# Rotary embedding on one core: the first and last rows move as f32 on SyncE's queue, and the positions come in four small transfers

## Chip, core and metric

The kernel runs on one core of a Trainium2 chip. The metric is the device time of one execution in microseconds, the median of three runs. The profile shows one execution; its span is a little shorter than the device time, because some of the launch and the end lies outside it.

## What is computed

`x` holds 8 x 8 heads of 1024 positions with 64 features in f32. Each position turns the two halves of its features by an angle, position times frequency:

```python
half = x.shape[-1] // 2                       # 32
angles = np.outer(positions, freqs)           # 1024 x 32
cos, sin = np.cos(angles), np.sin(angles)
x_first, x_second = x[..., :half], x[..., half:]
out_first  = x_first * cos - x_second * sin
out_second = x_first * sin + x_second * cos
```

The input is 16.8 MB of f32 and so is the output. The table of angles is small (1024 x 32) and is the same for all 64 heads.

## The kernel before

A partition holds 64 consecutive positions (`C = 64`) of one head, so 16 partitions (`chunks`) hold a head and a tile of 128 partitions holds 8 heads. There are 8 tiles (`ntiles`). A row of a tile is one position with its 64 features. Each partition's part of a tile is one run of 64 x 64 x 4 B = 16 KB in memory.

The transfers of `x` are issued by GpSimd, and they convert f32 to bf16 on the way in and bf16 to f32 on the way out. All eight loads are issued at once; each tile has buffers of its own.

```python
pos_i = singles.tile([P, C, 1], positions.dtype)
nc.sync.dma_start(out=pos_i, in_=...)      # positions, repeated for 8 groups of 16 partitions
fr = singles.tile([P, half], f32)
nc.scalar.dma_start(out=fr, in_=freqs[None, :].to_broadcast([P, half]))

xts = []
for g in range(ntiles):
    xt = xpool.tile([P, C, d], bf16)
    nc.gpsimd.dma_start(out=xt.rearrange("p c d -> p (c d)"), in_=hbm(x, g))
    xts.append(xt)
```

VectorE and ScalarE build the tables of sine and cosine, `sin_h` and `cos_h`, in bf16. The angle is counted in turns, the whole turns are taken off, and ScalarE applies the sine:

```python
nc.vector.tensor_copy(out=pos_f, in_=pos_i.bitcast(mybir.dt.int32)[:, :, :1])
...
nc.vector.tensor_mul(out=turns, in0=pos_f..., in1=fturn...)      # 128 x 2048, f32
nc.vector.tensor_scalar(out=whole, in0=turns, ...)               # rounded to whole turns
nc.vector.tensor_sub(out=turns, in0=turns, in1=whole)
nc.scalar.activation(out=sin_h, in_=turns, func=Sin, scale=twopi)
nc.scalar.activation(out=whole, in_=turns, func=Abs)
nc.scalar.activation(out=cos_h, in_=whole, func=Sin, scale=-twopi, bias=half_pi)
```

Then each tile takes six VectorE operations, and its store is issued by GpSimd:

```python
for g in range(ntiles):
    ...
    v.tensor_mul(out=t1, in0=xf, in1=sin_h)
    v.tensor_mul(out=t2, in0=xs, in1=sin_h)
    v.tensor_mul(out=of, in0=xf, in1=cos_h)
    v.tensor_mul(out=os_, in0=xs, in1=cos_h)
    v.tensor_sub(out=of, in0=of, in1=t2)
    v.tensor_add(out=os_, in0=os_, in1=t1)
    nc.gpsimd.dma_start(out=hbm(out, g), in_=ot.rearrange("p c d -> p (c d)"))
```

Of the kernel before, what the change touches and what calls it, by code (L numbers as in the profile page):

```python
# [2 lines left out]

# [4 lines left out]


@with_exitstack  # L10
def kernel(
    ctx: ExitStack,
    tc: tile.TileContext,
    x: bass.AP,
    freqs: bass.AP,
    positions: bass.AP,
    out: bass.AP,
):
    nc = tc.nc
    f32 = mybir.dt.float32  # L20
    bf16 = mybir.dt.bfloat16
    Sin = mybir.ActivationFunctionType.Sin
    Alu = mybir.AluOpType

    b, h, seq, d = x.shape
    bh = b * h
    half = d // 2
    P = 128
    twopi = 2 * math.pi


    C = 64
    chunks = seq // C
    group = P // chunks
    ntiles = bh // group
    run = C * d
    assert chunks * C == seq and group * chunks == P and ntiles * group == bh

    singles = ctx.enter_context(tc.tile_pool(name="singles", bufs=1))
    xpool = ctx.enter_context(tc.tile_pool(name="xin", bufs=ntiles))  # L40
    opool = ctx.enter_context(tc.tile_pool(name="xout", bufs=ntiles))
    tpool = ctx.enter_context(tc.tile_pool(name="tmp", bufs=2))

    def hbm(t, g):
        return bass.AP(tensor=t.tensor, offset=t.offset + g * P * run, ap=[[run, P], [1, run]])


    pos_i = singles.tile([P, C, 1], positions.dtype)
    nc.sync.dma_start(
        out=pos_i,  # L50
        in_=bass.AP(tensor=positions.tensor, offset=positions.offset,
                    ap=[[0, group], [C, chunks], [1, C]]))
    fr = singles.tile([P, half], f32)
    nc.scalar.dma_start(out=fr, in_=freqs[None, :].to_broadcast([P, half]))


    xts = []
    for g in range(ntiles):
        xt = xpool.tile([P, C, d], bf16)
        nc.gpsimd.dma_start(out=xt.rearrange("p c d -> p (c d)"), in_=hbm(x, g))  # L60
        xts.append(xt)


    half_pi = singles.tile([P, 1], f32)
    nc.vector.memset(half_pi, math.pi / 2)  # L65
    pos_f = singles.tile([P, C, 1], f32)
    nc.vector.tensor_copy(out=pos_f, in_=pos_i.bitcast(mybir.dt.int32)[:, :, :1])  # L67
    fturn = singles.tile([P, 1, half], f32)
    nc.vector.tensor_scalar_mul(out=fturn[:, 0, :], in0=fr, scalar1=1.0 / twopi)  # L69
    turns = singles.tile([P, C, half], f32)  # L70
    nc.vector.tensor_mul(out=turns, in0=pos_f.to_broadcast([P, C, half]),  # L71
                         in1=fturn.to_broadcast([P, C, half]))
    whole = singles.tile([P, C, half], f32)
    magic = 1.5 * 2.0 ** 23
    nc.vector.tensor_scalar(out=whole, in0=turns, scalar1=magic, scalar2=magic,  # L75
                            op0=Alu.add, op1=Alu.subtract)
    nc.vector.tensor_sub(out=turns, in0=turns, in1=whole)  # L77
    sin_h = singles.tile([P, C, half], bf16)
    cos_h = singles.tile([P, C, half], bf16)
    nc.scalar.activation(out=sin_h, in_=turns, func=Sin, scale=twopi)  # L80

    nc.scalar.activation(out=whole, in_=turns, func=mybir.ActivationFunctionType.Abs)  # L82
    nc.scalar.activation(out=cos_h, in_=whole, func=Sin, scale=-twopi, bias=half_pi)  # L83

    v = nc.vector
    for g in range(ntiles):
        xt = xts[g]
        xf = xt[:, :, :half]
        xs = xt[:, :, half:]
        ot = opool.tile([P, C, d], bf16)  # L90
        of = ot[:, :, :half]
        os_ = ot[:, :, half:]
        t1 = tpool.tile([P, C, half], bf16)
        t2 = tpool.tile([P, C, half], bf16)
        v.tensor_mul(out=t1, in0=xf, in1=sin_h)  # L95
        v.tensor_mul(out=t2, in0=xs, in1=sin_h)  # L96
        v.tensor_mul(out=of, in0=xf, in1=cos_h)  # L97
        v.tensor_mul(out=os_, in0=xs, in1=cos_h)  # L98
        v.tensor_sub(out=of, in0=of, in1=t2)  # L99
        v.tensor_add(out=os_, in0=os_, in1=t1)  # L100
        nc.gpsimd.dma_start(out=hbm(out, g), in_=ot.rearrange("p c d -> p (c d)"))  # L101


# [1 line left out]
_INS = ['x', 'freqs', 'positions']  # L105
_OUTS = [((8, 8, 1024, 64), 'float32')]


# [23 lines left out]
```

## Time and profile before

| what | value |
|---|---|
| device time | 86.46 us (86.45 to 86.51) |
| span of the profiled execution | 84.2 us |
| VectorE busy | 60.7 us in 54 instructions |
| ScalarE busy | 7.0 us |
| GpSimd busy (issuing transfers) | 8.9 us |
| one VectorE operation on a tile, 128x2048 bf16 | 1.22 us |
| loads, stores | 8 of each, all on GpSimd's queue |
| read from memory, written to memory | 16.86 MB, 16.78 MB |

How to read it: the engines run side by side, so the busy times do not add up. VectorE is ahead of its stores, which stand in a queue; a wait of an engine matters only if what it waits for is on the path that sets the end. The transfers' bytes are counted on the side they are written to, so a converting load counts 1 MB for 2 MB read. "To landing" is the time from the issue of a transfer to the signal that all of it has arrived, so it includes the time that it stood in the queue.

### The profile page before, as it was taken

What the parts mean: (1) busy time and instruction counts of PE and PEld (TensorE: products, weight loads), DVE (VectorE), ACT (ScalarE), POOL (GpSimd) and SP (SyncE); (2) the same over time, 40 slices, a digit from 0 to 9 for tenths busy, and PEclk for the clock granted to TensorE, in tenths of its full rate; (3) what the DMA queues carried; (4) which work ended last, traced back from release to release, by engine and by line L of the source; (5) the groups of instructions that cost most, each with busy time, mean ns of one, the idle gap of its engine ahead of it and who ended that gap; (6) DMA issues with size and microseconds to landing.
All of it is one profiled execution on the core that took longest, in us unless ns stands there. A gap on an engine that the chain in (4) does not pass through costs nothing.

```text
span 84.2 us, 132 instructions
## 1 busy us (share of the span) xinstructions
DVE 60.7 (72%) x54; ACT 7.0 (8%) x4; POOL 8.9 (11%) x20
## 2 busy tenths in 40 slices
DVE  0069927999999999999999999999999910000000
ACT  4100079900000000000000000000000000000000
POOL 5960000000201100200200200100020020000000
DMA  0399999999999999999999999999999999999990
GB/s 2 60 210 214 214 218 218 214 214 214 214 222 210 218 218 210 218 218 214 210 342 405 459 405 467 381 490 381 482 389 467 405 451 420 428 443 405 467 373 0
DMA packets 2584, 25.25 MB, mean 300 GB/s; under 512 B 408, under 2 KB 536, under 8 KB 536
## 3 DMA queue, kind: packets, MB, share of 16 engines
q0 software_dynamic: 2304, 25.17, 97.2%
q1 hardware_dynamic: 136, 0.07, 0.3%
q10 hardware_dynamic: 144, 0.02, 0.1%
HBM read 16.86 MB, written 16.78 MB: 399 GB/s over the span
## 4 chain that ended last, share of the span: by engine, by line
issue 65%; DMA 10%; POOL 4%; POOLq 1%; PEldq 0%
DMA xt<-in_x_dram 10%; POOL out_dram L101 4%; POOLq L127 1%; POOLq L101 0%; PEldq L127 0%
## 5 line engine op out<-in xcount | busy, mean ns | idle before, releaser
L95 DVE TENSOR_TENSOR t<-xt,sin_h 128x2048 bf16<-128x2048 bf16 x8 | 9.8, 1224 | 2.0 <-ACT sin_h L80 2.0
L101 POOL DMA_DIRECT2D out_dram<-ot x8 | 4.3, 535 | 58.6 <-DVE ot L100 58.6
L99 DVE TENSOR_TENSOR ot<-ot,t 128x2048 bf16<-128x2048 bf16 x8 | 9.8, 1225 | 0.0
L97 DVE TENSOR_TENSOR ot<-xt,cos_h 128x2048 bf16<-128x2048 bf16 x8 | 9.8, 1224 | 0.0
L100 DVE TENSOR_TENSOR ot<-ot,t 128x2048 bf16<-128x2048 bf16 x8 | 9.8, 1224 | 0.0
L98 DVE TENSOR_TENSOR ot<-xt,cos_h 128x2048 bf16<-128x2048 bf16 x8 | 9.8, 1223 | 0.0
L96 DVE TENSOR_TENSOR t<-xt,sin_h 128x2048 bf16<-128x2048 bf16 x8 | 9.8, 1223 | 0.0
L60 POOL DMA_DIRECT2D xt<-in_x_dram x8 | 4.4, 578 | 0.8 <-PEq L127 0.8
L67 DVE CAST pos_f<-pos_i 128x64 f32<-128x64 int32 x1 | 0.2, 196 | 4.1 <-DMA pos_i<-in_positions_dram 4.1
L80 ACT ACTIVATE sin_h<-turns 128x2048 bf16<-128x2048 f32 x1 | 1.9, 1911 | 8.7 <-DVE turns L77 8.7
L77 DVE TENSOR_TENSOR turns<-turns,whole 128x2048 f32<-128x2048 f32 x1 | 2.3, 2293 | 0.0
L71 DVE TENSOR_TENSOR turns<-pos_f,fturn 128x2048 f32<-128x2048 f32 x1 | 2.3, 2291 | 0.0
L83 ACT ACTIVATE cos_h<-whole,half_pi 128x2048 bf16<-128x2048 f32 x1 | 2.0, 2003 | 0.0
L82 ACT ACTIVATE whole<-turns 128x2048 f32<-128x2048 f32 x1 | 1.9, 1896 | 0.0
L80 ACT ACT_TABLE_LOAD x1 | 1.3, 1283 | 1.1 <-PEq L116 1.1
L75 DVE TENSOR_SCALAR whole<-turns 128x2048 f32<-128x2048 f32 x1 | 1.2, 1226 | 0.0
L65 DVE MEMSET half_pi<- 128x1 f32 x1 | 0.1, 59 | 0.8 <-PEq L116 0.8
L69 DVE TENSOR_SCALAR fturn<-fr 128x32 f32<-128x32 f32 x1 | 0.2, 174 | 0.0
L116 POOL MEMSET const-float32-0.0<- 128x1 f32 x1 | 0.1, 99 | 0.2 <-issue 0.2
L116 POOL MEMSET const-bfloat16-1.0<- 128x1 bf16 x1 | 0.1, 102 | 0.0
L116 POOL MEMSET const-float32-1.0<- 128x1 f32 x1 | 0.1, 99 | 0.0
L116 POOL MEMSET const-uint8-127<- 128x1 uint8 x1 | 0.1, 99 | 0.0
## 6 DMA issues: line engine op xcount, KB each, us to landing
out_dram<-ot POOLq DMA_DIRECT2D x8, 2048.0 KB, 21.7
xt<-in_x_dram POOLq DMA_DIRECT2D x8, 1024.0 KB, 23.6
pos_i<-in_positions_dram SPq DMA_DIRECT2D x1, 64.0 KB
fr<-in_freqs_dram ACTq DMA_DIRECT2D x1, 16.0 KB, 3.6
```

The lines of the kernel that those rows point to most:

```text
L60: nc.gpsimd.dma_start(out=xt.rearrange("p c d -> p (c d)"), in_=hbm(x, g))
L71: nc.vector.tensor_mul(out=turns, in0=pos_f.to_broadcast([P, C, half]), in1=fturn.to_broadcast([P, C, half]))
L77: nc.vector.tensor_sub(out=turns, in0=turns, in1=whole)
L80: nc.scalar.activation(out=sin_h, in_=turns, func=Sin, scale=twopi)
L83: nc.scalar.activation(out=cos_h, in_=whole, func=Sin, scale=-twopi, bias=half_pi)
L95: v.tensor_mul(out=t1, in0=xf, in1=sin_h)
L96: v.tensor_mul(out=t2, in0=xs, in1=sin_h)
L97: v.tensor_mul(out=of, in0=xf, in1=cos_h)
L98: v.tensor_mul(out=os_, in0=xs, in1=cos_h)
L99: v.tensor_sub(out=of, in0=of, in1=t2)
L100: v.tensor_add(out=os_, in0=os_, in1=t1)
L101: nc.gpsimd.dma_start(out=hbm(out, g), in_=ot.rearrange("p c d -> p (c d)"))
```

## The change

The change moves three things. The first 16 rows of every partition of tile 0 (the head) are loaded as f32 on SyncE's queue, in two transfers with 2 KB runs, and ScalarE converts them to bf16 into the tile. The last 24 rows of tile 7 (the tail) are computed into an f32 tile and stored on SyncE's queue, in three transfers with 2 KB runs. The positions, which were one transfer to all 128 partitions on SyncE, become four transfers of 16 partitions on ScalarE's queue, one to each quadrant of 32 partitions, and a shuffle on VectorE copies them to the other 16 partitions of the quadrant; the frequencies go to one partition of each quadrant and are shuffled likewise. Two memsets go ahead of these, since the shuffle reads partitions that no transfer fills.

Its purpose is to let data move before GpSimd's first transfer gets under way, and to end with short runs on another queue. Tile 1 is computed ahead of tile 0. The lines at the end hold SyncE's last transfers until the loads of the head and tables and the first seven stores are done.

```diff
-    pos_i = singles.tile([P, C, 1], positions.dtype)
-    nc.sync.dma_start(out=pos_i, in_=...)
-    fr = singles.tile([P, half], f32)
-    nc.scalar.dma_start(out=fr, in_=freqs[None, :].to_broadcast([P, half]))
+    xts = [xpool.tile([P, C, d], bf16, name="xt") for _ in range(ntiles)]
+    piece = 8
+    head = 2 * piece
+    x0 = singles.tile([P, head, d], f32)
+    for r in range(0, head, piece):
+        nc.sync.dma_start(out=x0[:, r:r + piece], in_=hbm(x, 0, r, r + piece))
+
+    pos_i = singles.tile([P, C, words], i32)
+    nc.vector.memset(pos_i, 0)
+    for q in range(0, P, 32):
+        nc.scalar.dma_start(out=pos_i[q:q + chunks].bitcast(positions.dtype), in_=...)
+    fr = singles.tile([P, half], f32)
+    nc.vector.memset(fr, 0.0)
+    nc.scalar.dma_start(out=fr[0:P:32], in_=freqs[None, :].to_broadcast([P // 32, half]))
 ...
-        nc.gpsimd.dma_start(out=xt.rearrange("p c d -> p (c d)"), in_=hbm(x, g))
+        lo = 0 if g else head
+        nc.gpsimd.dma_start(out=xts[g][:, lo:], in_=hbm(x, g, lo))
+
+    nc.vector.stream_shuffle(pos_i, pos_i, [i % chunks for i in range(32)])
+    nc.vector.stream_shuffle(fr, fr, [0] * 32)
 ...
+    nc.scalar.copy(out=xts[0][:, :head], in_=x0)
 ...
+    def rotate(g, lo, hi, ot):      # the six operations, on rows lo to hi
+        ...
+    tail = 3 * piece
+    ots = []
+    for g in [1, 0] + list(range(2, ntiles)):
+        hi = C if g < ntiles - 1 else C - tail
+        ot = opool.tile([P, C, d], bf16, name="ot")[:, :hi]
+        rotate(g, 0, hi, ot)
+        ots.append(ot)
+        nc.gpsimd.dma_start(out=hbm(out, g, 0, hi), in_=ot)
+
+    last = singles.tile([P, tail, d], f32)
+    rotate(ntiles - 1, C - tail, C, last)
+
+    sp = nc.sync
+    sp.keepalive_nop(ins=[sp.lower_ap(cos_h)])
+    for done in [pos_i, fr, x0] + ots[:-1]:
+        sp.clobber_nop(outs=[sp.lower_ap(done)])
+    for r in range(0, tail, piece):
+        lo = C - tail + r
+        tc.keep_in_program_order(
+            sp.dma_start(out=hbm(out, ntiles - 1, lo, lo + piece), in_=last[:, r:r + piece]))
+    sp.clobber_nop(outs=[sp.lower_ap(ots[-1])])
+    for r in range(0, tail - piece, piece):
+        sp.clobber_nop(outs=[sp.lower_ap(last[:, r:r + piece])])
```

## The prediction

> **What bounds the kernel now.** I read the page's slices first, then the queues, then a table of stages, and last who waited for whom. The page's part 2 gives the DMA engines' busy share and what they moved in 40 slices of 2.1 us; part 3 gives the queues:
>
> ```profile
> DMA  0399999999999999999999999999999999999990
> GB/s 2 60 210 214 214 218 218 214 214 214 214 222 210 218 218 210 218 218 214 210 342 405 459 405 467 381 490 381 482 389 467 405 451 420 428 443 405 467 373 0
> q0 software_dynamic: 2304, 25.17, 97.2%
> ```
>
> The DMA engines are full from the third slice to the last but one, and almost all their work is on GpSimd's queue. The two rates, about 215 and about 430 GB/s, are the same thing: the loads cast f32 to bf16 and the page counts the bf16 side, so 8.39 MB counted are 16.78 MB of f32; the stores are counted on the f32 side. On the f32 side the engines run at about 430 GB/s throughout. The stages show where they do not (columns: window, length, busy time of VectorE, ScalarE, GpSimd, PE clock, DMA share, GB/s):
>
> ```profile
> 1.00:2.00 1.00, 0.00 (x0) 0.86 (x1) 0.76 (x2) 1.00 0.02 3
> 2.00:3.00 1.00, 0.00 (x0) 0.42 (x1) 1.00 (x3) 1.00 0.32 52
> 3.00:4.00 1.00, 0.00 (x0) 0.00 (x0) 1.00 (x3) 1.00 0.40 54
> 4.00:5.00 1.00, 0.07 (x1) 0.00 (x0) 1.00 (x3) 1.00 0.88 186
> ...
> 20.00:40.00 20.00, 20.00 (x19) 0.00 (x0) 1.61 (x3) 1.00 1.03 216
> ...
> 44.00:60.00 16.00, 16.00 (x15) 0.00 (x0) 1.07 (x2) 1.00 1.06 432
> ...
> 81.00:82.00 1.00, 0.00 (x0) 0.00 (x0) 0.00 (x0) 1.00 0.96 393
> 82.00:83.00 1.00, 0.00 (x0) 0.00 (x0) 0.00 (x0) 1.00 0.04 0
> ```
>
> Two holes: up to about 4.0 us, and after 82.0. The timeline gives the issues, and the view of the tile `xt`, narrowed to the first load, its time to landing:
>
> ```profile
> 0.74 0.36 ACTq L54 DMA_DIRECT2D fr<-in_freqs_dram  x1
> 0.74 0.74 SPq L49 DMA_DIRECT2D pos_i<-in_positions_dram  x1
> 1.25 4.38 POOL L60 DMA_DIRECT2D xt<-in_x_dram  x8 [0.80 <-PEq L127]
> DMA to landing us min/median/max: 8.6/8.6/8.6
> ```
>
> Tile 0 is issued at 1.25 us and lands 8.6 later, at 9.8. The other landings, from the same view, are then evenly spaced: the last load 5.0 + 38.9 = 43.9 us, the eighth store 68.0 + 14.8 = 82.8 us. That is (82.8 - 9.8) / 15 = **4.87 us for each 2.10 MB tile**, or 431 GB/s, with no gap between loads and stores. The time is the start plus sixteen such steps plus an end: after 82.8 come 1.4 us of span, and 86.46 - 84.2 = 2.3 us lie outside the span.
>
> VectorE does not bound it. It has 60.7 us of work, and its last store is handed over at 68.0 and then queues for 14.8 us. The large wait in the list,
>
> ```profile
> POOL out_dram L101 <- DVE ot L100: 58.6, 8, 16.9
> ```
>
> costs nothing, because stores cannot start before the loads that stand ahead of them have gone by at about 43 us, and by then four stores are waiting.
>
> **What the Trainium skill says.** "DMA: Bandwidth & Descriptors", section Specifications, puts the fabric ceiling of a core's sixteen engines at 435 GB/s; the trace's 432 agrees, so the middle of this kernel can't be made faster by another order. The same page, "Issuing engines are not separate DMA queues", says that transfers of SyncE, ScalarE and GpSimd run on the same sixteen engines and interleave: a byte moved to SyncE's queue saves nothing by itself, only if it fills a hole. No run here has shown two busy queues yet. Its section "Anatomy of one DMA" says that engines do not wait on semaphores, only the issuing sequencer does, and that a completion waits for the receipt of the last byte; here the last bytes move at 82.0 and the store lands at 82.8. "ScalarE: Activation LUTs", "What ACT_TABLE_LOAD costs", gives 1283 ns for a table load; the page's row says 1283 as well.
>
> **The change, part by part.**
>
> *Head.* Rows 0 to 15 of tile 0 (128 x 16 x 64 x 4 B = 524 KB) leave GpSimd's transfer and go as f32, in two transfers on SyncE, issued first. At 431 GB/s they are 524 / 431 = 1.22 us of engine time. SyncE's first issue is at 0.74 and took 0.74 us for `pos_i`, ScalarE's took 0.36 for `fr`; both have 128 rows. I take 0.4 to 0.7 for each half of the head, so they are issued by 1.5 to 2.1 us. A finer look at the start shows the first bytes of `fr` at about 2.2, 1.45 us after its issue. So the halves move from 2.2 and from 2.6 to 2.9, 0.61 us each, and are done by about 3.5. GpSimd's own transfers begin to move at about 3.6 and reach their rate by 4.2. The head falls wholly into the hole: **-1.2 us**, as large as it can be. GpSimd's first load shrinks to three quarters and everything behind it on the queue comes 1.22 us earlier.
>
> *Positions and frequencies.* They shrink from 128 rows each to 64 and 4 rows. They took a third of the engines between 2 and 4 us, so the head meets less traffic than was there. They are issued on ScalarE behind a memset on VectorE, four and one transfers one after another. By rows, one of 16 rows would cost 0.09 us to issue; if the cost is per transfer, up to 0.7. Issued between 1.0 and 1.5 or 4.5, with 3.6 us to landing as `fr` had, they land at 5 to 8 instead of 4.9 us. Two shuffles add about 0.27 and 0.17 us (2291 ns for 2048 f32 elements is 1.12 ns each; the 32-element row of 174 ns leaves 0.14 fixed). So the tables come 0.5 to 3.5 us later. The first store is then handed over at 23 to 26 us, where it is not needed until 42. **0 on the path.**
>
> *ScalarE.* It gets a copy of 128x1024 (half of the 128x2048 row's 1.9 us, so 1.0) and a second table load of 1.28. With the head landed at about 4.5 it is ready for the sine at about 7, before the angles at 11.2 us. **0.**
>
> *VectorE's end.* Tile 7 is split. The 40-row part costs 6 x 1.14 x 40/64 = 4.3 us (1.14 is the distance of one start from the next); the 24-row part has four operations with f32 output, which I put at the 1.12 ns of the f32 rows: 4 x 0.86 + 2 x 0.43 = 4.3. Together 8.6 in place of 6.8. VectorE ends at about 70 to 73 us. SyncE waits for more than that, so **0**.
>
> *Tail.* The last 24 rows of tile 7 (786 KB, 1.83 us) go in three transfers on SyncE. SyncE is made to wait for the first seven stores to land. Tile 6 landed at 61.17 + 16.8 = 78.0; less 1.2 this is 76.8. GpSimd's last store is now 1.31 MB, 3.04 us. Its engines reach it about 0.9 us before tile 6's landing is signalled, at 75.9, and would be through at 78.9. SyncE's first piece, issued at 76.8, moves from about 78.3, when 0.6 us of store are left; the others follow every 0.4 to 0.7 us and take 0.61 each. The engines never run dry, by a margin of 0.6 us, and the bytes end at 75.9 + 3.04 + 1.83 = 80.8, which is 82.0 - 1.2. The tail saves no bytes. What it may bring is a finer end, 2 KB runs in place of 16 KB, so that sixteen engines finish together: the share is 0.96 in the last microsecond against 1.06, so 0.1 us, and at best some 0.2 more in the receipt. **-0.2 to +0.3**, centre 0.
>
> Sum: -1.2, rounded to 86.46 - 1.25 = **85.2 us**, or 1.5% faster.
>
> **Rivals.**
> 1. *The late gate.* If tile 6's completion reaches SyncE later than I think, or issues cost 0.7 or more each and their first bytes take over 2 us, the store is through before the pieces arrive and the engines idle for 0.3 to 0.8 us at the end. For it: 0.6 us is a thin margin and three issues are in series. Against it: 24 rows and not more look chosen to leave room. It makes 85.6 to 86.0.
> 2. *The head does not fit.* 2 KB runs at a pitch of 16 KB may run slower than 430 GB/s, or share the engines with GpSimd's first packets after 3.6 us. At half rate only half is gained: 85.8. The hole being there whatever happens, it can't be a loss by itself.
> 3. *The end is shorter than I count.* The 0.8 us from last byte to landing and 1.4 us from landing to the end of the span were measured with a GpSimd transfer last. If a SyncE transfer of short runs is acknowledged sooner, 0.3 to 0.6 us more go: 84.6 to 84.9, around the 2% line. Nothing in this trace says so; `fr`, on a like queue, took 3.6 us to land.
> 4. *It is hidden anyway.* If GpSimd's queue were limited by its descriptors and not by the engines, the head would gain nothing. Against it: all eight loads are issued by 5.6 us and take until 43.9.
>
> **Range and chances.** The head's gain is arithmetic on a hole that the trace shows, so most of the mass lies between 84.9 and 85.6; the end widens it on both sides. 8 in 10: 84.5 to 86.0. Faster by 2% is under 84.73 and needs the third rival: 0.2. Slower by 2% would need a stall of over 3 us: 0.02. Within 2%: 0.78.
>
> **What the profile after would show.** DMA share near full from about 2.3 us; `x0` landed by 4.5; the first load on GpSimd's queue landed at about 8.6 in place of 9.8; the other landings 4.87 apart; tile 6's store landed at 76.8; the share with no dip between 78 and 81; last bytes at 80.8, span 83.0. The first view that differs names the failed step: an early hole still open (rival 2), a dip near 79 (rival 1), a span that ends under 2 us after the last byte (rival 3). A slower steady rate than 431 GB/s, from two queues at once, would make the whole sum wrong.

## The result and the profile after

The changed kernel takes **85.57 us** (median of 4 runs, 85.30 to 86.10) against 86.48 before (86.45 to 86.63). The ratio is 0.990, with a 95% interval of 0.985 to 0.995: about 1% faster. The predicted 85.2 us lies 0.4 below the median, and the stated range holds the result. The sum behind it was wrong all the same: almost none of the gain is where the prediction put it, so the agreement is largely luck. The profiled execution, 85.30 us, is the fastest of the four.

From the page of the changed kernel, the slices of DMA share (2.1 us each) and the queues:

```profile
DMA  1999999999999999999999999999999999999990
q0 software_dynamic: 2304, 24.12, 94.4%
q1 hardware_dynamic: 720, 1.31, 4.9%
```

The second slice is now full, as intended, and 1.31 MB (head and tail) go on SyncE's queue, `q1`. The table of stages after (window, length, busy time of VectorE, ScalarE and GpSimd, PE clock, DMA share, GB/s):

```profile
2.00:3.00 1.00, 0.00 (x0) 0.00 (x0) 1.00 (x3) 1.00 0.90 202
3.00:4.00 1.00, 0.00 (x0) 0.00 (x0) 1.00 (x3) 1.00 0.84 222
...
44.00:60.00 16.00, 16.00 (x16) 0.00 (x0) 1.59 (x3) 1.00 1.06 429
...
79.00:80.00 1.00, 0.00 (x0) 0.00 (x0) 0.00 (x0) 1.00 0.95 348
...
81.00:82.00 1.00, 0.00 (x0) 0.00 (x0) 0.00 (x0) 1.00 0.57 217
```

Between 2 and 4 us the share rose from 0.36 to 0.87, the steady rate is the same 430 GB/s, and the engines run out about half a microsecond earlier. The view of `xt` after, narrowed to the first load, and then the timeline and the view of `last`, narrowed to the tail's last piece:

```profile
DMA to landing us min/median/max: 7.9/7.9/7.9
```

```profile
78.62 1.13 SPq L141 DMA_DIRECT2D out_dram<-last  x1
DMA to landing us min/median/max: 4.0/4.0/4.0
```

Tile 0 lands 0.7 us earlier than before (1.25 + 7.9 = 9.15). The last landing of all, 78.62 + 4.0 = 82.6 us, is only 0.2 earlier than the 82.8 of before, and that in the fastest of the four executions. Yet the device time of this execution is 1.13 us below that of the profiled execution before. So I split both executions in three:

| part | before | after | difference |
|---|---|---|---|
| start to the last landing | 82.83 | 82.63 | -0.20 |
| last landing to the end of the span | 1.41 | 0.89 | -0.52 |
| end of the span to the device time | 2.19 | 1.77 | -0.42 |

Nine tenths of a microsecond come after the last byte has landed. Two theories of it, both about the end of the program, were put to the test: **W**, that SyncE's early waits shorten the end, and **T**, that the tail's last transfers do. The prediction's own sum, all from the head, was the third.

### The profile page after: what moved, and what is told of

It is laid out like the page before. It is cut to its first block, busy times and chain, and to the rows that moved or that the text cites. A ratio compares the mean times of both kernels' runs of the same rounds, so it can differ in the third digit from the quotient of the medians.

```text
span 83.5 us, 169 instructions
## 1 busy us (share of the span) xinstructions
DVE 63.5 (76%) x66; ACT 9.3 (11%) x6; POOL 8.8 (11%) x20
## 3 DMA queue, kind: packets, MB, share of 16 engines
q1 hardware_dynamic: 720, 1.31, 4.9%
## 4 chain that ended last, share of the span: by engine, by line
DVE 75%; DMA 8%; ACT 2%; ACTq 2%; DVEq 1%; issue 1%
DVE t L114 11%; DVE t L115 11%; DVE ot L117 10%; DVE ot L119 10%; DVE ot L118 10%; DVE ot L116 10%; DMA pos_i<-in_positions_dram 8%; DVE turns L87 3%; DVE turns L93 3%; ACT sin_h L96 2%; ACTq L63 2%; DVE whole L91 1%; DVEq L170 1%; DVE last L117 1%; DVE last L118 1%; DVE last L116 1%
## 5 line engine op out<-in xcount | busy, mean ns | idle before, releaser
L114 DVE TENSOR_TENSOR t<-xt,sin_h 128x2048 bf16<-128x2048 bf16 (+2 forms) x9 | 9.9, 1097 | 2.0 <-ACT sin_h L96 2.0
L115 DVE TENSOR_TENSOR t<-xt,sin_h 128x2048 bf16<-128x2048 bf16 (+2 forms) x9 | 9.9, 1097 | 0.0
L117 DVE TENSOR_TENSOR ot<-xt,cos_h 128x2048 bf16<-128x2048 bf16 (+1 forms) x8 | 9.3, 1165 | 0.0
L119 DVE TENSOR_TENSOR ot<-ot,t 128x2048 bf16<-128x2048 bf16 (+1 forms) x8 | 9.3, 1165 | 0.0
L118 DVE TENSOR_TENSOR ot<-ot,t 128x2048 bf16<-128x2048 bf16 (+1 forms) x8 | 9.3, 1164 | 0.0
L116 DVE TENSOR_TENSOR ot<-xt,cos_h 128x2048 bf16<-128x2048 bf16 (+1 forms) x8 | 9.3, 1164 | 0.0
L101 ACT CAST xt<-x 128x1024 bf16<-128x1024 f32 x1 | 1.0, 1044 | 0.0
L119 DVE TENSOR_TENSOR last<-last,t 128x768 f32<-128x768 f32 x1 | 0.9, 949 | 0.0
L117 DVE TENSOR_TENSOR last<-xt,cos_h 128x768 f32<-128x768 bf16 x1 | 0.9, 948 | 0.0
L116 DVE TENSOR_TENSOR last<-xt,cos_h 128x768 f32<-128x768 bf16 x1 | 0.9, 947 | 0.0
L118 DVE TENSOR_TENSOR last<-last,t 128x768 f32<-128x768 f32 x1 | 0.9, 947 | 0.0
```

What stands on the lines that cost most here:

```text
L101: nc.scalar.copy(out=xts[0][:, :head], in_=x0)
L114: v.tensor_mul(out=t1, in0=xf, in1=sin)
L115: v.tensor_mul(out=t2, in0=xs, in1=sin)
L116: v.tensor_mul(out=of, in0=xf, in1=cos)
L117: v.tensor_mul(out=os_, in0=xs, in1=cos)
```

## The experiments

Each kernel is compared with the kernel before on the same chip; its median there was 86.35 to 86.40 us. The changed kernel itself was not run again beside these kernels, so a comparison with its 85.57 is one of the ratios. Medians and ranges are of all runs; three slow ones (87.05, 87.08 and 86.58 us, in experiments 2, 3 and 10), each over 1.5% above the fastest of its kernel, are left out of the ratios. "Signals" are the sixteen completion signals that the trace has for a transfer, read here as one from each DMA engine; their times, like the first and last times of packets below, are read from the trace's single records.

**1. SyncE's waits alone.** Added to the kernel before:

```diff
+    ots = []
 ...
+        ots.append(ot)
 ...
+    sp = nc.sync
+    sp.keepalive_nop(ins=[sp.lower_ap(cos_h)])
+    for done in [pos_i, fr] + ots:
+        sp.clobber_nop(outs=[sp.lower_ap(done)])
```

> The kernel before with one thing of the change: SyncE waits for the tables and each of the eight stores in turn ahead of the end of the program. No head, no tail, positions as before. Theory W (most of the gain is the end of the program, which is shorter because SyncE has taken its waits one by one before the last store lands): 85.6 to 85.9 us, last store still landing at 82.8, and less than 1.0 us of span after it. Theory T (the end is shorter because a SyncE transfer of short runs is last): 86.4 to 86.5, 1.4 us of span after the landing. The prediction's own sum (all from the head): 86.4 to 86.5.

Measured: 86.38 us, ratio 1.000 (0.999 to 1.001). Theory W fell. The reason stands in the view of the program's closing line, which lists the DRAIN instructions of GpSimd and SyncE (durations in ns as min/median/max, first and last start in us):

```profile
L134 POOLq DRAIN  x3: 39/87/15623, 67.6 to 83.7; - x3
L134 SPq DRAIN  x3: 7/7/13, 82.6 to 83.5; - x3
```

GpSimd's first DRAIN starts after its last issue at 67.64 and lasts 15.62 us, to 83.27. The last store had landed at 82.57, and SyncE was through its waits at 82.65. So GpSimd, not SyncE, is last, by 0.6 us; shortening SyncE's list changes nothing. The same view of the kernel before and then of the changed kernel:

```profile
L127 POOLq DRAIN  x3: 39/90/15564, 68.0 to 84.0; - x3
```

```profile
L170 POOLq DRAIN  x3: 39/108/11062, 70.4 to 83.3; - x3
L170 SPq DRAIN  x3: 7/7/7, 82.7 to 83.0; - x3
```

Before, the drain ends at 67.97 + 15.56 = 83.53, 0.70 us after the last landing. After, it ends at 70.36 + 11.06 = 81.42, which is 0.7 us after the landing of GpSimd's own last store at 80.73; SyncE's last piece lands at 82.63 and SyncE is through at 82.71. The new theory, **D**: GpSimd's drain ends 0.7 us after its last transfer has landed, and the tail hides that by having SyncE's transfers land later.

**2. Head and positions alone.** The changed kernel with eight whole stores on GpSimd and no lines for SyncE at the end.

> Head and positions as in the change; eight whole stores on GpSimd, no tail and no waits of SyncE. The prediction's sum: 85.2 us, all of the gain. Theory W: the head is worth only what the landings of the loads show, 0.5 us, so 85.9 to 86.0, with the last store landing at about 82.3 and 1.4 us of span after it. Theory T: the same 85.9 to 86.0.

Measured: 86.17 us, ratio 0.997 (0.995 to 0.998), with a scatter of 85.55 to 87.05. The head does not bring 1.2, and not 0.5. First, 0.4 of what lies outside the span is gone here too (1.77 in place of 2.19), without any tail; experiment 5 takes that up. The last landing is 82.90 us, no earlier than before. The stages of the kernel before, and then of this one, show how that can be:

```profile
81.00:81.50 0.50, 0.00 (x0) 0.00 (x0) 0.00 (x0) 1.00 0.88 360
81.50:82.00 0.50, 0.00 (x0) 0.00 (x0) 0.00 (x0) 1.00 1.04 426
82.00:82.50 0.50, 0.00 (x0) 0.00 (x0) 0.00 (x0) 1.00 0.08 0
```

```profile
81.00:81.50 0.50, 0.00 (x0) 0.00 (x0) 0.00 (x0) 1.00 0.52 197
81.50:82.00 0.50, 0.00 (x0) 0.00 (x0) 0.00 (x0) 1.00 0.19 66
82.00:82.50 0.50, 0.00 (x0) 0.00 (x0) 0.00 (x0) 1.00 0.01 0
```

With the head most engines are done by 81.5, so the head did take bytes off them. But the landing is the last of the sixteen signals. Before, the last store's signals came from 82.48 to 82.83; here from 81.49 to 82.90. The fastest engine gained 1.0 us and the slowest nothing. Their mean came at 81.99 against 82.62 before, and against 82.31 in experiment 1, where loads and stores are those of the kernel before: 0.3 to 0.6 us earlier, not 1.2. The spread is there from the first load (8.41 to 9.76, against 9.21 to 9.80) and does not close: it is 1.35 us there, 1.3 at the last load and 1.4 at the last store.

**3. Head, positions and waits, no tail.**

> Head, positions and SyncE's waits, eight whole stores on GpSimd, no tail. Theory W, with the tail losing about 0.3 us by its late start: 85.0 to 85.2, below the changed kernel's 85.57. Theory T: 85.9 to 86.0, as without the waits. The prediction's sum: 85.2.

Measured: 86.17 us, ratio 0.998 (0.996 to 1.000), like the head alone. Signals from 81.51 to 82.90 again, and GpSimd's drain to 83.60.

**4. Tail alone**, with SyncE's waits, positions and tile 0 as before.

> Tail with SyncE's waits; no head, positions as before. Theory W: the end is shorter by 0.6 to 0.9 but the tail's late start costs about 0.3, so 85.9 to 86.2, worse than the waits alone. Theory T: the end is shorter by the tail itself, 85.9 to 86.0, better than the waits alone (86.4). The prediction's sum: 86.2 to 86.5.

Measured: 85.70 us (85.57 to 85.84), ratio 0.991 (0.988 to 0.993): the whole of the changed kernel's gain, within the intervals. The last landing is even 0.3 us later than before (83.13 against 82.83); the gain is all in the end, 0.87 us of span after the landing in place of 1.41, and 1.77 outside in place of 2.19. GpSimd's drain ended at 81.94, before SyncE's last landing, as theory D has it.

**5. Ten idle instructions on VectorE.** The 0.4 us outside the span had gone from kernels with a head and from kernels with a tail, but not from the kernel with the waits alone. What the first two share is a longer VectorE program. The queue view of the kernel before, for the time after the span, has one record:

```profile
q14 instruction: 1, 0.01, 0.5%
```

It is an 8 KB instruction fetch at 85.92 us. In every kernel with a longer VectorE program it came in mid-run. Theory **F**: the late fetch is what costs the 0.4 us. So, in the kernel before:

```diff
+    pad = singles.tile([P, 1], f32)
+    for _ in range(10):
+        nc.vector.memset(pad, 0.0)
```

> The kernel before with ten memsets of one element per partition added on VectorE, nothing else. They do no work that is used. Theory F (0.4 us of the gain of every kernel with a longer VectorE program lies outside the span, because an 8 KB instruction fetch that came at 85.9 us, after the span, now comes at about 57 us): the fetch moves to about 57 us, 1.8 us outside the span in place of 2.2, device time 86.0 to 86.2, as in the kernel with the head alone. Theory that all of the tail's gain is its last transfers: 86.36, no change.

Measured: 85.97 us (85.87 to 86.05), ratio 0.995 (0.994 to 0.997). The memsets' results are not used. The fetch stands at 42.3 us, in the queue view of 42 to 43 us:

```profile
q14 instruction: 1, 0.01, 2.3%
```

and 1.79 us lie outside the span. Theory F holds: **0.4 us, nearly half of the change's gain, come from the program being longer**, not from anything that the change was written for. It holds in all fourteen kernels: 1.77 to 1.79 us outside the span in the twelve with the fetch in mid-run, 2.19 and 2.20 in the two with the fetch after it. That the fetch is VectorE's own is inferred; the record does not name the engine. The expected instant, 57 us, was off by 15 us, and why is open. Against this 85.97, the head and positions of experiments 2 and 3 (86.17), which have the fetch in mid-run too, bring nothing.

**6. The changed kernel without the head.**

> The changed kernel without the head: positions in four transfers, shuffles, tail and SyncE's waits; tile 0 loaded whole on GpSimd. If the head is worth nothing and the positions nothing: 85.6 to 85.8, like the tail alone (85.70). If the head is worth 0.5 us and the positions cost that much by spreading the engines: 86.0 to 86.2.

Measured: 85.69 us (85.55 to 85.78), ratio 0.992 (0.990 to 0.993), the same as the tail alone. Positions in four transfers bring nothing and cost nothing that these runs can tell, and tile 0's signals stay together (8.97 to 9.60). The changed kernel, with the head, is at 85.57 in four runs that reach from 85.30 to 86.10: no difference can be claimed.

**7. The changed kernel with positions as one transfer**, and the frequencies too, to 128 partitions on ScalarE.

> The changed kernel with positions and frequencies as one transfer each to 128 partitions, both on ScalarE, no shuffles; head and tail kept. If the head's gain is lost because the small transfers hold up some of the sixteen engines (the signals of tile 0's load spread over 1.4 us in the kernel with head and positions): 84.9 to 85.2, a spread of at most 0.7. If it is lost to the head's own two transfers: 85.5 to 85.7 or slower, with the same spread of 0.9 to 1.4.

Measured: 86.12 us (85.87 to 86.39), ratio 0.997 (0.996 to 0.998), and tile 0's signals from 8.46 to 9.86. So the small transfers do not spread the engines; beside the head they are the better form, by some 0.5 us. The head goes with the spread.

**8. The tail issued early.**

```diff
-    for done in [pos_i, fr, x0] + ots[:-1]:
+    for done in [pos_i, fr, x0]:
```

> The changed kernel without SyncE's waits for the first seven stores: the three pieces of the tail are issued when VectorE is done, at about 74.5 us, and land before GpSimd's last store, which is then the last transfer again. Theory D (GpSimd's drain ends 0.7 us after its own last store has landed, and the tail gains by having that happen earlier than the end): the drain is last again, so 0.5 to 0.6 us slower than the changed kernel, 86.0 to 86.2. Theory that short runs at the end even out the engines, in whatever place: 85.5. Theory that the gate costs time: 85.2 to 85.4.

Measured: 85.73 us (85.16 to 86.10), ratio 0.992 (0.989 to 0.995), not different from the changed kernel. The expectation that GpSimd's store would now be last was wrong, so this is no further test of D. The timeline has the issues at 74.8 us, and the queue view of 75 to 79 us shows what moved:

```profile
74.81 1.32 SPq L141 DMA_DIRECT2D out_dram<-last  x3
```

```profile
q0 software_dynamic: 158, 1.68, 106.0%
```

For over four microseconds no packet of SyncE's moved, while 158 of GpSimd's did. Between 79 and 83 us the order is reversed:

```profile
q1 hardware_dynamic: 432, 0.79, 51.9%
q0 software_dynamic: 39, 0.24, 16.0%
```

Most of what stood in GpSimd's queue went first. SyncE's first packet of the tail starts at 79.30 us here and at 79.30 in the changed kernel, where it is issued 2.9 us later. The gate on SyncE therefore costs nothing, and the tail would be last without it.

**9. Memsets ahead of the tables, with the tail alone**, to move the fetch to where the engines are idle.

```diff
+    for _ in range(26):
+        nc.vector.memset(pos_f[:, :1], 0.0)
+        nc.vector.memset(fturn[:, :, :1], 0.0)
```

> The tail alone (no head, positions as before) with 52 one-element memsets on VectorE ahead of the tables, which do no useful work. They should move VectorE's 8 KB instruction fetch from 58 us, where the sixteen engines are full, to about 3 us, where they are not. If the fetch delays the one engine that carries it by its 0.34 us, and that engine then ends last, the signals of the last piece come within 0.4 us of each other in place of 0.8, and the time is 85.3 to 85.5 in place of 85.70. If the fetch in mid-run costs nothing: 85.7.

Measured: 85.62 us (85.54 to 85.75), ratio 0.991 (0.989 to 0.994). The fetch came at 13.2 us, not at 3, so it still met full engines; the last signals came within 0.5 us (82.42 to 82.90) in place of 0.8. The time is 0.08 below the tail alone, inside the scatter: a fetch in mid-run costs little, at most.

**10. A head of 8 rows**, one transfer (`head = piece`).

> The changed kernel with a head of 8 rows, one transfer of 2 KB runs, in place of 16 rows in two. If the late engines come from the second transfer's packets, which meet those of GpSimd's first load: the slowest engine gains too, spread of tile 0's signals at most 0.7 us, 85.1 to 85.3 (0.6 us of head, less than 16 rows would bring in full). If a head's gain goes to the fast engines whatever its size: 85.5 to 85.7.

Measured: 85.92 us (85.26 to 86.58), ratio 0.994 (0.992 to 0.996). The head had wholly landed at 0.74 + 3.0 = 3.7 us, and still tile 0's signals spread from 8.09 to 9.78. So the second transfer is not the cause of the spread. Their mean, 8.76, is as early as with 16 rows.

**11. The 16 rows in one transfer**, 4 KB runs.

> The changed kernel with the same 16 rows of head in one transfer of 4 KB runs. If the loss lies in the serial issue of two transfers with 2 KB runs: 84.9 to 85.2 and a head that has landed on all engines by 3.7 us. If it lies in the slowest engine, whatever the transfer: 85.5 to 85.7, with signals of tile 0's load still spread over 0.7 to 1.4 us.

Measured: 86.39 us (86.15 to 87.33), ratio 1.002 (1.000 to 1.003): the gain is gone. The head landed at 5.3 us, and tile 0's signals came from 8.66 to 10.40. Two transfers of 2 KB runs are the better form. A slowest engine that is clearly earlier than without a head shows in only two of the traces with a head: the changed kernel's and experiment 8's.

**12. The version that the runs point to.** The tail alone with 16 rows (`tail = 2 * piece`), and 34 rounds of the memsets of experiment 9.

> The version that the runs point to: no head, positions as before, a tail of 16 rows in two transfers on SyncE (1.2 us of bytes, more than the 0.7 us by which GpSimd's drain ends after its last store lands), SyncE's waits, and 68 one-element memsets on VectorE so that its instruction fetch comes in the first microseconds. Theory D with F: GpSimd's drain still ends before SyncE's last landing, the fetch is at 3 to 6 us, last landing at 82.6 to 82.9, 85.3 to 85.5 us, at or a little below the changed kernel's 85.57 and with a narrower scatter. If a drain that ends only 0.1 to 0.5 us ahead of SyncE's last landing still costs time, or a second fetch appears: 85.8 to 86.1.

Measured: 85.47 us (85.36 to 85.78), ratio 0.989 (0.987 to 0.991). It has no head, no copy on ScalarE and no positions in parts, and it is as fast as the changed kernel; it does not clearly beat it. The drain ended at 82.56, the last landing was at 83.12, the fetch at 7.7 us.

## Why the prediction came out right, point by point

- **What bounds the kernel**: right. The steady rate is 430 GB/s in every kernel, and VectorE's lateness (it ends at 74.5 us, later than the 70 to 73 of the prediction, and its first store is issued at 27.4 in place of 23 to 26) cost nothing.
- **Head, -1.2 us**: this step failed, in two places. First, "the head falls wholly into the hole". The prediction had GpSimd's transfers begin to move at 3.6 us and the head done by 3.5. The queue views, of 2 to 4 us before, in experiment 6 and after, then of 4 to 5 us and of 0 to 6 us after:

```profile
q0 software_dynamic: 7, 0.06, 26.2%
q1 hardware_dynamic: 68, 0.03, 5.8%
q10 hardware_dynamic: 120, 0.01, 4.1%
```

```profile
q0 software_dynamic: 20, 0.16, 87.0%
```

```profile
q0 software_dynamic: 2, 0.01, 4.9%
```

```profile
q1 hardware_dynamic: 51, 0.08, 25.1%
```

```profile
q1 hardware_dynamic: 288, 0.52, 33.0%
```

  The third of the engines that the prediction put down to positions and frequencies was mostly GpSimd's (`q0`: 26.2%, against 5.8% and 4.1%). In experiment 6, with neither the head nor the old positions, GpSimd's packets take 87.0%, though they move only 0.16 MB (0.33 on the f32 side). Their first packet starts at 2.6 to 2.8 us in the seven traces without a head and in that with 8 rows, at 3.6 to 4.1 in the six with 16 rows. The head itself takes 33.0% of 6 us, 1.98 us of each engine in place of 1.22, and its last packet ends at 4.8; it landed at 1.2 + 4.0 = 5.2, not by 4.5. So part of what the head moves early stands in the place of GpSimd's own first packets: the mean of tile 0's signals is 8.7 to 8.9 us in the changed kernel and experiments 2, 3 and 8, against 9.2 to 9.5 in the seven without a head, 0.3 to 0.8 earlier and not 1.2.

  Second, the step went from the mean to the end of the program, and the end is set by the slowest of sixteen. How late the slowest is differs between executions of one and the same start: its signal for tile 0 came at 9.76 and 9.80 us in experiments 2 and 3, at 9.30 in experiment 8 and at 9.10 in the changed kernel's profile, its fastest run, where 0.5 us of the head is left at the last load. So the head adds scatter: 85.55 to 87.05 in 22 runs of the head alone, against 86.21 to 86.84 in 59 of the kernel before. Its median worth is 0.1 us or less, with the tail (85.57 and 85.73 against 85.69 and 85.70), and without the tail it is none (86.17 against the 85.97 of experiment 5).
- **Positions, 0 on the path**: right. Each issue of 16 rows took 0.44 us, nearer to the estimate per transfer than to the 0.09 by rows, and the tables came 4.8 us late (their first use by VectorE starts at 17.90 us, before at 13.10), more than the 0.5 to 3.5 predicted. The view of `pos_i`, its issues and the landings:

```profile
L63 ACTq DMA_DIRECT2D pos_i<-in_positions_dram x4: 442/443/450, 1.0 to 2.4; - x4
DMA to landing us min/median/max: 3.0/5.8/6.5
```

  The last landed at about 8.9 us, against the 5 to 8 that were predicted.
- **ScalarE, 0**: right. Copy and second table load (1.28 us, as "ScalarE: Activation LUTs" of the Trainium skill, section "What ACT_TABLE_LOAD costs", has it) were done at 8.9, before the angles at 16.0.
- **Tail, -0.2 to +0.3**: mis-sized, and its sign was open. Alone it brought 0.7 us (ratio 0.991). Of that, in the profiled execution, 0.4 is the fetch and 0.5 the hidden drain, less the 0.3 by which its last piece lands later.
- **Rival 1, the late gate**: tile 6's store landed at 77.7, later than the 76.8 predicted, but the gate has no cost (experiment 8).
- **Rival 2, the head does not fit**: right as far as the mean goes: the head took 1.6 times the engine time reckoned for it, and it met GpSimd's first packets. That the runs of 2 KB make it slower is not shown: in one transfer of 4 KB runs it took 1.9 us as well. The spread is not in this rival.
- **Rival 3, the end is shorter**: right in size (0.3 to 0.6 us; 0.52 measured in the span). Its sign, "a span that ends under 2 us after the last byte", told nothing: the last packet ends 1.4 us before the end of the span, but it did so by 1.8 before, at 82.46 and not at the 82.0 that the prediction read. Its reason, short runs that are acknowledged sooner, was not what the runs show: the tail's last piece is signalled 0.5 us after the last packet (0.4 for the last store before, where the prediction had 0.8), and what ends sooner is GpSimd's drain.
- **Rival 4, hidden anyway**: no. With the head the mean signal of the last load came at 42.8 to 43.0 us, without it at 43.4 to 43.7.
- The predicted 85.2 was thus a head's gain that for the most part did not come, in the place of an end's gain that was not counted. That the two are of like size is luck.

**Left open**: why some engines gain nothing from the head, and why its packets take so long. The spread comes from neither the second transfer nor the positions. The records of packets don't name their engine, so the slow one can't be followed. That the drain's lag is what the tail hides rests on the ends of the drain in all kernels (0.69 to 0.70 us after GpSimd's last landing, hidden or not), on the ends of the span (in all fourteen traces 0.7 to 0.8 us after the later of GpSimd's long drain and SyncE's first closing DRAIN) and on experiment 4; a kernel in which GpSimd ends last beside a tail was meant by experiment 8 and not obtained.

## What to carry to other kernels

Where transfers bound a kernel, fill a hole only after asking whose packets already move in it and what the slowest of the sixteen engines does: the landing is the last of their signals, and a mean share near 1 shows neither. Split the time of any change into landing, end of the span and outside of it, and take the ends apart before believing in a mechanism: here the end gave all of the gain. If GpSimd's queue carries the last stores, try giving the last microsecond of bytes to another queue, so that its drain is over when they land; here 1.2 us of bytes were enough (experiment 12).

## What the runs showed of the hardware

- GpSimd's long closing DRAIN ends 0.69 to 0.70 us after its last transfer has landed, in each of the fourteen traces.
- An instruction fetch of 8 KB after the span costs 0.4 us of device time; ten idle instructions that bring it forward win that back (86.40 to 85.97).
- SyncE's packets, issued at 74.8 us in experiment 8, moved only from 79.3 us, behind most of what GpSimd had queued. "DMA: Bandwidth & Descriptors" of the Trainium skill, section "Queues, rings and completion order", says that an engine goes round the queues it has work for, packet by packet; this trace shows none of that for four microseconds, and the measurement decides. When SyncE's work reached the engines it does not show.
- The frequencies' transfer, 128 runs of 128 B, took 10.2 us to land in experiment 7, beside a head and behind the positions, and 3.6 us in the kernel before.
- With 16 rows of f32 moving first on SyncE's queue, GpSimd's first packet starts at 3.6 to 4.1 us; without, at 2.6 to 2.8.
